# Order of the last stage: a plain tile between two difference jobs, and one quarter's job behind the plain tiles

## The chip, the cores and the metric

The kernel runs on one core of a Trainium2 chip. The metric is the device time of one execution in microseconds; lower is better. The core has TensorE (PE, with its weight loads PEld), VectorE (DVE), ScalarE (ACT), GpSimd (POOL) and SyncE (SP), each with an instruction queue of its own; SyncE issues nearly all DMA transfers.

## The reference

One pre-norm layer for 512 tokens of width 1024, all in float32: a mixing block (attention, pooling and a state-space branch, gated and added to `x`), then a feed-forward block with a short causal convolution, then a last RMSNorm. The change touches only the end:

```python
def conv_ffn(u, w_up, conv_w, conv_b, w_down):
    h = causal_dwconv(u @ w_up, conv_w, conv_b)      # 512 x 5632
    a, v = h[..., :D_FF], h[..., D_FF:]               # D_FF = 2816
    return (jax.nn.silu(a) * v) @ w_down              # 2816 x 1024
...
    x = x + conv_ffn(rmsnorm(x, ln2_g[i]), ...)
return rmsnorm(x, final_g)
```

## The kernel before

**Split products.** Every large product is made in a reduced-precision float format with both operands split in a rounded part and a remainder: `mm3` issues rounded x rounded, rounded x remainder and remainder x rounded weights, in that order (line 234). A weight tile passes through the same steps each time. `fetch` loads it into one of two `raw` buffers (line 183, SyncE). `cast` rounds it in two parts into `wh`, one of three buffers (line 195, ScalarE). `low` subtracts to get the remainder `wl`, one of two buffers (line 215, VectorE); with that `raw` is free again.

**Jobs.** The program is a list of jobs, one for each weight tile, in the order of `program`. Ahead of the body of job n the main loop emits the split of job n+1 (`low`), the rounding of job n+2 (`cast`, with the job's `form` ahead of it, and its two parts emitted in the next calls of `step`) and the load of job n+3 (`fetch`). Each engine runs what it is given in exactly the order in which it is written, so the order of the list sets the order on all queues. `step` also advances the generators in `running`, which emit small pieces of later work.

**The down projection.** The 22 row blocks of `w_down` (128 rows each) are taken in three parts. Two groups of eight blocks are each computed as a 2 x 2 block product with seven products in place of eight, from sums and differences of activation halves and weight quarters (`sevens_down`); the jobs are named `one` to `seven`. The last six blocks are taken plainly (`blocks_of`), once for the left 512 columns (h = 0) and once for the right ones (h = 1): a job with four blocks and one with two, each for four tiles of 128 tokens (tb = 0 to 3). A job of the seven has 2 x 12 matmuls of 512 columns; the plain jobs have 48 and 24.

The second group's jobs `two`, `one`, `five` and `six` stand between and behind the last jobs of the up projection; `seven`, `four` and `three` and the plain jobs make up the last stage, `down`. Jobs `one`, `six`, `seven` and `four` accumulate into the same two banks `X`, one after the other; after each, `plus` (line 1218, VectorE) adds what the banks then hold to a part of the residual `X1[tb, h]`. The difference weights come from `form`, a subtraction by `diff` on VectorE (line 339) ahead of the rounding:

```python
seven = job(q(0, 0), side(3), into(X, "p7", lambda i: [(2 + i, 1)]),
            lambda: diff(seven.raw, W[1], seven.raw))
four = job(q(1, 0), side("A22"), into(X, "p4", lambda i: [(2 + i, 0)]),
           lambda: diff(four.raw, four.raw, W[1]))
```

So `seven` serves the right half's lower quarter (tb 2 and 3, h = 1) and `four` the left half's lower quarter (tb 2 and 3, h = 0). `three` leaves its sums in two further banks, which the right half's plain jobs continue for tb 0 and 1.

**The last norm** needs the sum of squares of both halves of a token tile. `early` emits the left half's part (`norm_early`: squares on ScalarE, line 438; a small row on VectorE, line 461; the product with the norm's weight on GpSimd, line 462) one `step` after the left half of the tile is complete. `norm_late` follows the right half's evacuation (line 1370) tile by tile, and stores the tile (line 1379).

Of the kernel before, what the change touches and what calls it, by code (L numbers as in the profile page):

```python
# [83 lines left out]
def trunk(ctx: ExitStack, tc, out, x, rel_bias, ln1_g, w_in, b_gate, w_a, pool_w, pool_scale, w_b,  # L84
# [26 lines left out]
    def MM(name):  # L111
        return psum.tile([P, S], F32, name=name, tag="mm")

    def SM(name):
        return psum.tile([P, S], F32, name=name, tag="sm")
# [9 lines left out]
    waiting, running = [], []  # L125
# [99 lines left out]
    def wsrc(w, k0, k1, c0, c1):  # L225
        return w[k0 * P:k1 * P, c0:c1].rearrange("(k p) c -> p k c", p=P)
# [111 lines left out]
    def diff(out, a, b):  # L338
        dve.tensor_tensor(out, a, b, OP.subtract)  # L339
        return out  # L340
# [116 lines left out]
    def norm_early(t, g):  # L457

        ss, v0, xg = small("ss", [P, 1]), cpool.tile([P, 1], F32, name=f"v0_{len(V0)}"), T("xg")
        squares(act, t, ss)  # L460
        dve.tensor_scalar(v0, ss, 1.0 / D, EPS, OP.mult, OP.add)
        pool.tensor_tensor(xg, t, g[:, :S], OP.mult)
        V0.append(v0)
        return v0, xg

    def norm_late(t, g, v0, outs, both=False):

        ss, v, sq, r, rt = (small(n, [P, 1]) for n in ("ss", "v", "sq", "r", "rt"))
        squares(act, t, ss)
        xg = T("xg")  # L470
        dve.tensor_tensor(xg, t, g[:, S:], OP.mult)
        dve.scalar_tensor_tensor(v, ss, 1.0 / D, v0, OP.mult, OP.add)
        act.activation(sq, v, AF.Sqrt)
        yield xg
        dve.reciprocal(r, sq)
        dve.scalar_tensor_tensor(rt, r, v, r, OP.mult, OP.mult)
        dve.tensor_scalar(rt, rt, -0.5, 1.5, OP.mult, OP.add)
        if both:
            dve.tensor_tensor(r, r, rt, OP.mult)
            (_, a), (_, b) = outs(xg)  # L480
            dve.tensor_scalar(a, a, r, None, OP.mult)
            act.mul(b, b, r)
            return
        for o, src in outs(xg):
            dve.tensor_scalar(o, src, r, rt, OP.mult, OP.mult)
# [731 lines left out]
    def plus(tb, h, what):  # L1217
        dve.tensor_tensor(X1[tb, h], X1[tb, h], what, OP.add)
# [4 lines left out]
    def second_half(p, tb):  # L1223
        return [t[:, tb * P:(tb + 1) * P] for t in ACTS[2 * p + 1]]

    def sums(j, p, i):
        return [t[:, i * P:(i + 1) * P] for t in FS[j, p]]

    def quarters(g):

        base = g * KG * P
        q = lambda two, h: w_down[base:base + KG * P, h * S:(h + 1) * S].rearrange(
            "(k two p) c -> two p k c", two=2, p=P)[two]
        n2 = KG // 2
        ks = [g * n2 + i for i in range(n2)]

        def product(ps, ws, parts, first, last, again):
            wh, wl = ws
            mm3(ps, lambda k: wh[:, k, :], lambda k: wl[:, k, :], lambda k: parts[k][0],
                lambda k: parts[k][1], range(n2), first, last, flip=True, again=again)  # L1240

        def job(source, side, use, form=None):
            def body(ws):
                for i in range(2):
                    parts = [side(p, i) for p in ks]
                    use(i, lambda ps, first=True, last=True, again=False:
                        product(ps, ws, parts, first, last, again))
                    step()
            j = Job([source] if source is not None else [], n2, S, body)
            j.form = form  # L1250
            if source is None:
                j.load = lambda: None
            return j

        return q, job

    def side(j):
        if j == "A11":
            return first_half
        if j in ("A12", "A22"):  # L1260
            return lambda p, i: second_half(p, i + 2 * (j == "A22"))
        return lambda p, i: sums(j, p, i)

    def into(banks, name, adds, first=False, close=True):
        def use(i, product):
            if first:
                banks[i] = SM(name)
            product(banks[i], first, close, not first)
            for tb, h in adds(i):
                plus(tb, h, banks[i])  # L1270
        return use

    def sevens_down(g, keep=False):

        q, job = quarters(g)
        W, X, Z = [], {}, {}

        def load():
            for h in range(2):
                W.append(ypool.tile([P, 4, S], F32, name="w3", tag="xs"))  # L1280
                sp.dma_start(W[h], q(h, 1))

        two = job(q(1, 0), side("A12"), into(Z, "p2", lambda i: [(i, 0)], True))
        one = job(q(0, 0), side("A11"), into(X, "p1", lambda i: [(i, 0)], True))
        one.then = lambda: diff(W[0], W[0], one.raw)
        five = job(None, side(1), into(Z, "p5", lambda i: [(2 + i, 1)], True), lambda: W[0])
        if keep:
            three = job(q(1, 1), side(4), into(Z, "p3", lambda i: [], close=False))
            six = job(None, side(2), into(X, "p6", lambda i: [(i, 1)]), lambda: diff(W[1], W[1], W[0]))
        else:  # L1290
            three = job(None, side(4), into(Z, "p3", lambda i: [(i, 1)]), lambda: W[1])
            three.then = lambda: diff(W[1], W[1], W[0])
            six = job(None, side(2), into(X, "p6", lambda i: [(i, 1)]), lambda: W[1])
        seven = job(q(0, 0), side(3), into(X, "p7", lambda i: [(2 + i, 1)]),
                    lambda: diff(seven.raw, W[1], seven.raw))
        four = job(q(1, 0), side("A22"), into(X, "p4", lambda i: [(2 + i, 0)]),
                   lambda: diff(four.raw, four.raw, W[1]))
        return load, dict(two=two, one=one, five=five, three=three, six=six, seven=seven, four=four), Z

    def down(rest, opened):  # L1300

        plain = blocks_of(0, {}, (), ())
        yield rest["seven"]
        yield next(plain)
        yield rest["four"]
        yield from plain
        yield rest["three"]
        yield from blocks_of(1, opened, (0, 1), ())

# [53 lines left out]
    def early(tb):  # L1363
        yield
        fin[tb] = norm_early(X1[tb, 0], fin["g"])

    def blocks_of(h, acc, opened, keep):
        def evac(tb, ps):
            t = X1[tb, h]
            dve.tensor_tensor(t, t, ps, OP.add)  # L1370
            if h == 0:
                running.append(early(tb))
                return
            v0, xg0 = fin[tb]
            for _ in norm_late(t, fin["g"], v0, lambda xg1: ((xg1, xg1), (xg0, xg0)),
                               tb == 3):
                xg1 = _
            for i, o in ((1, xg1), (0, xg0)):
                (sp if i or tb < 3 else act).dma_start(out[tb * P:(tb + 1) * P, i * S:(i + 1) * S], o)

        return jobs_b(lambda k0, k1: [wsrc(w_down, KS + k0, KS + k1, h * S, h * S + S)], S,
                      lambda k, tb: ACTS[KS + k][0][:, tb * P:(tb + 1) * P],
                      lambda k, tb: ACTS[KS + k][1][:, tb * P:(tb + 1) * P], KF - KS, evac,
                      mk=(MM, SM)[h], tail=2 if h else 0, acc=acc, opened=opened, keep=keep,
                      again=(0, 1) if h else ())
# [6 lines left out]
    def program():  # L1392
# [34 lines left out]
        for pair in range(2):  # L1427
            for h in range(2):
                yield from wo_jobs(pair, h)
            if pair == 0:  # L1430
                yield Call(ff_cols)
        first, between, _ = sevens_down(0)
        second_, last_, opened = sevens_down(1, keep=True)
        extra = {EARLY + i: between[w] for i, w in enumerate(
            ("two", "one", "five", "three", "six", "seven", "four"))}
# [9 lines left out]
        yield Call(lambda: fin.setdefault("g", grow(final_g)))  # L1445
        yield Call(finish)
        yield from down(last_, opened)

    jobs = list(program())
# [19 lines left out]
    first = [MM("pa") for _ in range(4)]  # L1469
# [57 lines left out]
    banks = [SM("uT") for _ in range(4)]  # L1527
# [137 lines left out]
```

## Time and profile before

| | |
|---|---|
| median of 3 runs | 1039.03 us (1038.7 to 1039.3) |
| profiled execution | 1038.0 us |
| its span | 1036.2 us |
| mean granted TensorE clock | 0.998 |
| TensorE busy | 1024.7 us of the span (99%), 5204 matmuls |
| VectorE, ScalarE, GpSimd busy | 676.2, 473.8, 149.6 us |

The span runs from the first to the last recorded instruction; the execution's own time is 1.8 us longer. All times within the profile are counted from the span's start. Matmuls are pipelined: the next one begins before the last one's recorded end, and a row with "x4" is four in a run. The name after the line is what an instruction writes, and behind the arrow what it reads.

The last stage begins at about 978 us, with job `seven`.

### The profile page before, as it was taken

What the parts mean: (1) busy time and instruction counts of PE and PEld (TensorE: products, weight loads), DVE (VectorE), ACT (ScalarE), POOL (GpSimd) and SP (SyncE); (2) the same over time, 40 slices, a digit from 0 to 9 for tenths busy, and PEclk for the clock granted to TensorE, in tenths of its full rate; (3) what the DMA queues carried; (4) which work ended last, traced back from release to release, by engine and by line L of the source; (5) the groups of instructions that cost most, each with busy time, mean ns of one, the idle gap of its engine ahead of it and who ended that gap; (6) DMA issues with size and microseconds to landing.
All of it is one profiled execution on the core that took longest, in us unless ns stands there. A gap on an engine that the chain in (4) does not pass through costs nothing.

```text
span 1036.2 us, 13090 instructions
## 1 busy us (share of the span) xinstructions
PE 1024.7 (99%) x5204; PEld 859.7 (83%) x5204; DVE 676.2 (65%) x907; ACT 473.8 (46%) x765; POOL 149.6 (14%) x125
## 2 busy tenths in 40 slices
PE   9999999999999999999999999999999999999997
PEld 9898878898888878888888888898888888888785
DVE  6553566684356658766768656766768677666855
ACT  6432544442564364557445324545444443443332
POOL 1770000000000004210152500001111001111110
PEclk9999999999999999999999999999999999999999
DMA  8344312126222344542244525543233224323232
GB/s 280 123 131 134 116 47 75 31 64 200 82 82 82 98 132 115 144 136 69 66 149 153 172 82 204 175 140 114 82 115 122 89 82 163 122 90 114 82 122 82
DMA packets 119069, 120.76 MB, mean 117 GB/s; under 512 B 5316, under 2 KB 101383, under 8 KB 119008
## 3 DMA queue, kind: packets, MB, share of 16 engines
q1 hardware_dynamic: 118415, 119.07, 36.4%
q8 instruction: 41, 0.67, 0.3%
q10 hardware_dynamic: 592, 0.86, 0.2%
q14 instruction: 21, 0.16, 0.1%
HBM read 116.12 MB, written 2.22 MB: 114 GB/s over the span
## 4 chain that ended last, share of the span: by engine, by line
PE 96%; DVE 1%; ACT 1%; DMA 1%; issue 0%; ACTq 0%; DVEq 0%
PE pa L234 35%; PE pu L234 22%; PE pb L234 11%; PE pqk L234 9%; PE p L234 8%; PE pa L1516 2%; PE ps L670 1%; PE pu L1324 1%; PE ppw L234 1%; PE pt L698 1%; PE po L711 1%; PE py L996 1%; DMA xin<-in_x_dram 1%; PE pyo L1003 1%; PE pst L982 0%; PE pxs L950 0%
## 5 line engine op out<-in xcount | busy, mean ns | idle before, releaser
L215 DVE TENSOR_TENSOR wl<-raw,wh 128x2048 fp32r<-128x2048 f32 (+3 forms) x95 | 218.8, 2305 | 50.2 <-ACT wh L195 40.6
L195 ACT CAST wh<-raw 128x1024 fp32r<-128x1024 f32 (+3 forms) x188 | 189.4, 1026 | 68.0 <-DVE raw L339 26.0
L1187 DVE SCALAR_TENSOR_TENSOR hc<-pu,fcol,hc 128x510 f32<-128x510 f32 x88 | 65.8, 747 | 58.9 <-ACT hc L1184 57.3
L234 PE MATMUL pa<-uh,wh 128*128 128x512 f32 x384 | 98.5, 398 | 0.0
L234 PE MATMUL pa<-ul,wh 128*128 128x512 f32 x384 | 94.9, 389 | 0.0
L234 PE MATMUL pa<-uh,wl 128*128 128x512 f32 x384 | 94.9, 389 | 0.0
L234 PEld LDWEIGHTS pa<-ul,wh 128*128 128x128 f32 x384 | 72.1, 188 | 15.2
L234 PEld LDWEIGHTS pa<-uh,wl 128*128 128x128 f32 x384 | 72.1, 188 | 15.0
L234 PE MATMUL pu<-uh,wl 128*128 128x512 f32 (+1 forms) x352 | 83.7, 380 | 0.0
L234 PE MATMUL pu<-uh,wh 128*128 128x512 f32 (+1 forms) x352 | 83.5, 379 | 0.0
L234 PE MATMUL pu<-ul,wh 128*128 128x512 f32 (+1 forms) x352 | 83.5, 379 | 0.0
L234 PEld LDWEIGHTS pa<-uh,wh 128*128 128x128 f32 x384 | 70.3, 188 | 14.7 <-issue 0.7
L234 PEld LDWEIGHTS pu<-uh,wl 128*128 128x128 f32 x352 | 64.1, 188 | 12.8 <-DVE wl L215 0.3
L234 PEld LDWEIGHTS pu<-ul,wh 128*128 128x128 f32 x352 | 64.2, 188 | 12.5
L234 PEld LDWEIGHTS pu<-uh,wh 128*128 128x128 f32 x352 | 64.1, 188 | 12.4
L1192 POOL TENSOR_TENSOR hc<-hc 128x512 f32<-128x512 f32 x22 | 30.5, 1388 | 278.9 <-DVE hc L1187 243.1
L1184 ACT ACTIVATE hc<-pu,fcol,fcol 128x512 f32<-128x512 f32 x40 | 31.2, 780 | 81.3 <-PE pu L234 81.0
L958 POOL TENSOR_TENSOR xd<-xc,dec 128x512 f32<-128x512 f32 x6 | 6.4, 1060 | 334.1 <-DVE xc L952 315.2
L1085 ACT ACTIVATE sg<-pa,col 128x512 f32<-128x512 f32 x24 | 16.5, 688 | 55.3 <-PE pa L234 48.6
L691 ACT ACTIVATE sb<-sb,both 128x128 f32<-128x128 f32 (+1 forms) x72 | 30.1, 419 | 23.5 <-DVE both L688 13.4
L234 PE MATMUL pqk<-uh,wh 128*128 128x512 f32 x144 | 36.9, 394 | 0.0
L234 PE MATMUL pqk<-ul,wh 128*128 128x512 f32 x144 | 36.3, 390 | 0.0
(352 smaller groups left out, 1793.2 us busy)
## 6 DMA issues: line engine op xcount, KB each, us to landing
raw<-in_w_in_dram SPq DMA_DIRECT2D x25, 1024.0 KB
raw<-in_ffn_w_up_dram SPq DMA_DIRECT2D x22, 1024.0 KB
raw<-in_ffn_w_down_dram SPq DMA_DIRECT2D x11, 1024.0 KB
raw<-in_w_in_dram SPq DMA_DIRECT2D x20, 512.0 KB
raw<-in_w_o_dram SPq DMA_DIRECT2D x8, 1024.0 KB
raw<-in_w_b_dram SPq DMA_DIRECT2D x4, 1024.0 KB
al<-ad SPq DMA_DIRECT2D x16, 256.0 KB
w<-in_ffn_w_down_dram SPq DMA_DIRECT2D x4, 1024.0 KB
```

The lines of the kernel that those rows point to most:

```text
L195: act.copy(job.high[:, :, o], job.raw[:, :, o])
L215: (eng or dve).tensor_tensor(l[:, :, o], job.raw[:, :, o], h[:, :, o].bitcast(F32), OP.subtract)
L234: pe.matmul(ps, l, r, start=first and n == 0, stop=last and n == total - 1, skip_group_check=again)
L670: pe.matmul(pss[i][:, o:o + w * P], q[r, n * P:(n + 1) * P], k[r, kb * P:(kb + w) * P], start=True, stop=True)
L691: act.activation(sb[:, off:off + w * P], sb[:, off:off + w * P], AF.Exp, bias=nm[:, n, h:h + 1], accum_out=ls[:, n, h:h + 1])
L698: pe.transpose(pt[:, o:o + P], sb[:, o:o + P], eye)
L711: pe.matmul(po[DH * hh:DH * hh + DH, n * P:(n + 1) * P], V[g, kb + i][:, (2 * cc + hh) * DH:(2 * cc + hh + 1) * DH], probs[2 * cc + hh, mb ...
L1085: act.activation(s, ps, AF.Sigmoid, bias=col[:, o:o + 1])
L1184: act.activation(t, ps, AF.Identity, bias=ff["c1"][:, ff["b"] + m:ff["b"] + m + 1], scale=fw(2, m))
L1187: dve.scalar_tensor_tensor(t[:, sh:], ps[:, :S - sh], fw(k, m), t[:, sh:], OP.mult, OP.add)
L1192: pool.tensor_tensor(a, a, t, OP.mult)
L1516: pe.matmul(first[2 * n + j][:, lo:hi], a[:, k, j * P:(j + 1) * P], b[:, k, lo:hi], start=a is wh and b is uh and k == 0, stop=a is wl and ...
```

## The change

The first plain job of the left half (four blocks, all four token tiles) moves ahead of `seven`, between it and `six`, and `four` moves behind the second plain job. The order of the last stage becomes

| | |
|---|---|
| before | (six) seven, plain 4, four, plain 2, three, right half |
| after | (six) plain 4, seven, plain 2, four, three, right half |

Loads, casts, differences and splits move with their jobs. Since the left halves of tiles 2 and 3 are now completed by `four`, its `plus` and no longer the plain evacuation hands those two tiles to `early`.

```diff
-    def into(banks, name, adds, first=False, close=True):
+    def into(banks, name, adds, first=False, close=True, final=False):
...
             for tb, h in adds(i):
                 plus(tb, h, banks[i])
+            if final:
+                running.append(early(2 + i))
...
-        four = job(q(1, 0), side("A22"), into(X, "p4", lambda i: [(2 + i, 0)]),
+        four = job(q(1, 0), side("A22"), into(X, "p4", lambda i: [(2 + i, 0)], final=keep),
                    lambda: diff(four.raw, four.raw, W[1]))
...
         plain = blocks_of(0, {}, (), ())
+        yield next(plain)
         yield rest["seven"]
-        yield next(plain)
+        yield from plain
         yield rest["four"]
-        yield from plain
         yield rest["three"]
         yield from blocks_of(1, opened, (0, 1), ())
...
             if h == 0:
-                running.append(early(tb))
+                if tb < 2:
+                    running.append(early(tb))
                 return
```

## The prediction

> **What bounds the kernel now.** I read the page first, then TensorE's waits, then a table of stretches of the last stage, then its timeline engine by engine, because the page only says that TensorE is the bound and not where it loses time.
>
> ```profile
> span 1036.2 us, 13090 instructions
> PE 1024.7 (99%) x5204; PEld 859.7 (83%) x5204; DVE 676.2 (65%) x907; ACT 473.8 (46%) x765; POOL 149.6 (14%) x125
> ```
>
> TensorE is busy for 99% of the span, so a change of order can only win back its few gaps. TensorE's waits from 840 to 1030 us are a single row (time, count, longest), and the stretches cut at the job borders (length, then busy us and instructions of PE, PEld, DVE, ACT, POOL; granted clock; DMA share; GB/s) show the same gap:
>
> ```profile
> PE p L234 <- DVE x L1218: 1.7, 1, 1.7
> ...
> 978.16:980.04 1.88, 0.16 (x2) 0.03 (x1) 1.88 (x3) 0.59 (x1) 0.00 (x0) 1.00 0.00 0
> 980.04:985.60 5.56, 5.56 (x25) 4.58 (x25) 4.36 (x4) 0.00 (x0) 0.00 (x0) 1.00 0.72 236
> 985.60:996.48 10.88, 10.88 (x50) 9.01 (x48) 4.67 (x4) 3.11 (x5) 0.00 (x0) 1.00 0.35 122
> 996.48:1012.58 16.10, 16.10 (x73) 13.33 (x72) 10.88 (x13) 7.64 (x14) 6.89 (x4) 1.00 0.30 98
> 1012.58:1029.30 16.72, 16.70 (x74) 13.51 (x72) 10.37 (x25) 4.07 (x10) 0.20 (x1) 1.00 0.17 65
> 1029.30:1036.20 6.90, 0.00 (x0) 0.00 (x0) 2.72 (x8) 1.65 (x4) 0.00 (x0) 0.72 0.39 150
> ```
>
> Between 978.16 and 980.04 TensorE does nothing but drain; from 980.04 to 1029.30 it has no gap at all, and the clock is 1.00 on both sides. What remains after 1029.30 is the last tile's norm and its store. The timeline at the gap says who is late (start, length, engine, line, operation, count, and in brackets the idle time before):
>
> ```profile
> 972.72 1.07 PE L234 MATMUL p<-wh,sah 128*128 128x512 f32 x4
> ...
> 977.25 1.07 PE L234 MATMUL p<-wl,sah 128*128 128x512 f32 x4
> 980.04 1.17 PE L234 MATMUL p<-wh,sbh 128*128 128x512 f32 x4 [1.72 <-DVE x L1218]
> ...
> 985.60 1.07 PE L234 MATMUL pb<-wh,fh 128*128 128x512 f32 x4
> ...
> 969.41 2.29 DVE L339 TENSOR_TENSOR raw<-w,raw 128x2048 f32<-128x2048 f32 x1
> 971.61 1.53 DVE L1187 SCALAR_TENSOR_TENSOR hc<-pu,fcol,hc 128x510 f32<-128x510 f32 x2
> ...
> 975.30 0.69 DVE L1200 TENSOR_TENSOR fl<-hc,fh 128x512 fp32r<-128x512 f32 x1
> 975.91 3.38 DVE L215 TENSOR_TENSOR wl<-raw,wh 128x2048 fp32r<-128x2048 f32 x1
> ...
> 979.22 0.67 DVE L1218 TENSOR_TENSOR x<-x,p 128x512 f32<-128x512 f32 x1
> ...
> 973.60 1.04 ACT L195 CAST wh<-raw 128x1024 fp32r<-128x1024 f32 x1
> 974.65 0.62 ACT L1199 CAST fh<-hc 128x512 fp32r<-128x512 f32 x1
> ```
>
> Job "six" (sah) runs from 972.72. Job "seven" (sbh) accumulates into the same two banks (`X`), so its first matmul must wait until `plus` (L1218) has read six's first bank. The bank is complete at about 975.5, when three of six's six groups are done, but in VectorE's queue `plus` stands behind the split of seven's weights (L215, 975.91 to 979.29) and ends only at 979.89.
>
> **The change, part by part.** *The gap.* A job of 24 matmuls takes 5.44 us where nothing disturbs it, one of 48 takes 10.88; the chain of waits (start, length, what) has both:
>
> ```profile
> 956.56 5.44 PE p L234 x24
> ...
> 985.76 10.88 PE pb L234 x48
> 996.64 5.44 PE p L234 x24
> 1002.08 5.44 PE pb L234 x24
> ```
>
> Six could hand over at 972.72 + 5.44 = 978.16. Seven starts at 980.04, which is 1.88 us late, and itself takes 985.60 - 980.04 = 5.56, that is 0.12 more than 5.44, since the pipe has to fill again. So the gap costs 2.00 us. After the change the first plain job follows six. It writes four banks of its own (`pb`), does not need `X`, and its inputs, activations 16 to 19, were split long before. What it needs is its weights. Its rounded half is cast where seven's was (second part at 973.60), and its remainder is now the subtraction at VectorE's same place: behind the row at 975.30, ready at 979.29. The first remainder matmul is the ninth, after 8 x 5.44/24 = 1.81 us, at 979.97. That leaves 0.68 us of slack, so no wait: minus 2.00 us. The work itself, 24 + 48 + 24 + 24 matmuls, is unchanged.
>
> *Seven, one job later.* Its difference (L339, 2.29) leaves the place at 969.41 and stands behind the plain job's subtraction, 979.29 to 981.6; the `hc` row at 971.61 comes some 2 us earlier, which nobody waits for. Then come seven's first cast on ScalarE (1.04, to 982.6) with the last activation's cast queued behind it, six's two `plus` (to 984.5), the second cast (984.2), and seven's subtraction to about 986.9. Seven now starts at 978.16 + 10.88 = 989.04 and needs the remainder at 990.85: 4 us of slack. The plain job covers all of this; without such cover it would cost 986.9 - 979.97 = 7 us.
>
> *The loads.* Two raw buffers alternate, so each load starts when a subtraction frees its buffer. The issues on SyncE and what landed:
>
> ```profile
> 979.37 0.37 SPq L183 DMA_DIRECT2D raw<-in_ffn_w_down_dram  x1
> 983.32 0.37 SPq L183 DMA_DIRECT2D raw<-in_ffn_w_down_dram  x1
> ...
> 984.49 2.29 DVE L339 TENSOR_TENSOR raw<-raw,w 128x2048 f32<-128x2048 f32 x1 [1.20 <-DMA raw<-in_ffn_w_down_dram]
> 991.25 0.37 SPq L183 DMA_DIRECT2D raw<-in_ffn_w_down_dram  x1
> 996.41 2.00 ACT L195 CAST wh<-raw 128x1024 fp32r<-128x1024 f32 x2 [6.47 <-DMA raw<-in_ffn_w_down_dram]
> 1005.04 0.37 SPq L183 DMA_DIRECT2D raw<-in_ffn_w_down_dram  x1
> 1008.76 0.62 ACT L195 CAST wh<-raw 128x512 fp32r<-128x512 f32 x1 [1.78 <-DMA raw<-in_ffn_w_down_dram]
> ```
>
> So 1 MB is usable 5.12 to 5.16 us after its issue, half of that after 3.72. SyncE's queue keeps its length; only who takes which buffer changes. After the change the second plain job's load (0.5 MB) goes at 979.3 and lands at 983.0. Job four's load goes at 986.9, behind seven's subtraction, and lands at 992.1, when VectorE has nothing else urgent: its difference ends at 994.4, its two casts (2.00) at 996.4, its subtraction at 998.8. Four starts at 989.04 + 5.44 + 5.44 = 999.92 and needs the remainder at 1001.73: slack 2.9. Queued behind four's difference on VectorE are seven's two `plus`, and behind its subtraction the four evacuations of the plain jobs; their readers come later than 1001.7. The second plain job's own remainder waits only for a buffer that the first plain job frees at 989.0, and is needed at 994.48 + 0.9.
>
> *The norm's first half.* Tiles 2 and 3 now finish with four's `plus` instead of the plain evacuation, so their squares move behind four, while tiles 0 and 1 stay where they were. The rows that price this:
>
> ```profile
> 1005.64 0.63 ACT L438 ACTIVATE junk<-x 128x512 f32<-128x512 f32 x1 [0.59 <-DVE x L1370]
> 1005.69 7.10 POOL L462 TENSOR_TENSOR xg<-x,grow 128x512 f32<-128x512 f32 x4 [28.54 <-DVE x L1370]
> ...
> 1007.56 0.69 DVE L1370 TENSOR_TENSOR x<-x,pb 128x512 f32<-128x512 f32 x1 [0.67 <-PE pb L234]
> ...
> 1008.29 3.34 DVE L215 TENSOR_TENSOR wl<-raw,wh 128x2048 fp32r<-128x2048 f32 x1
> ```
>
> Four ends at 1005.36 and three at 1010.80, 2.00 us earlier than before. Job three's load goes at 990.4, lands by 997 and is split from 1001.9, behind four's split and the plain evacuations (four at 0.69, the last at 1001.6), to 1005.3, taking 3.34 if GpSimd's products lie beside it; needed at 1007.2. The right half's first load goes at 998.8 and lands at 1004.0; its casts end at 1006.0; tile 2's square (0.63) is queued behind them on ScalarE, tile 2's small `v0` row waits for it on VectorE, and behind that stands the right half's subtraction: from 1007.1, by 1010.5 at 3.34. It is needed at 1010.80 + 1.81 = 1012.6. The last half-load goes at 1005.3, lands at 1009.0, is cast around tile 3's square by 1011 and split by 1012.4; needed at 1010.80 + 2.72 + 0.9 = 1014.4. The thinnest slack is 2.0 us. I take nothing for all this; the bounds are nothing below, since unbroken matmuls can't be done earlier, and the second rival's price above.
>
> *A rule that speaks against it.* GpSimd's two products at the gap lie beside VectorE's work:
>
> ```profile
> 973.31 1.30 POOL L1192 TENSOR_TENSOR hc<-hc 128x512 f32<-128x512 f32 x1 [28.92 <-DVE hc L1187]
> 975.44 1.71 POOL L1192 TENSOR_TENSOR hc<-hc 128x512 f32<-128x512 f32 x1 [0.82 <-ACT fh L1199]
> ```
>
> The subtraction took 3.38 beside the second product, against 2.29 for the like-sized row at 969.41. The Trainium skill, page "SBUF — State Buffer", section "Who interferes with whom", says that a VectorE instruction with two SBUF inputs and a GpSimd instruction that reads SBUF exclude each other for a whole instruction. By that rule a further product beginning ahead of the subtraction's turn would hold it up once more; the first rival has that time, from rows. The row's extra 1.09 fits one such block, and no run shows two.
>
> *Sum.* -2.00 on TensorE, nothing elsewhere, the same tail: span 1036.2 - 2.0 = 1034.2, the profiled execution 1038.0 - 2.0 = 1036.0. The three timed runs have a median of 1039.03 (1038.7 to 1039.3), 1.0 above the profiled one; from it 1037.03. I predict 1037.0.
>
> **Rivals.** *A new wait takes part of the gain.* If both products fall on the plain job's subtraction, it ends some 1.3 later, at 980.6, and TensorE waits 0.6 plus a refill of 0.12: gain 1.3, time 1037.7. Against: the first product is freed by the `hc` row that now comes earlier, at about 971, away from it.
>
> *Loads too slow, the time ends above.* After the change the loads of four and three are issued 3.5 us apart, and each later one hangs on the split before it. If a load needed L instead of 5.2 us, four's split would end at 998.8 + (L - 5.2), the right half's load would start there and take L, and its casts (2.00) and its split (2.29) would follow; that split is needed at 1012.6. It costs from 2L = 14.7, at some 7.4 us a load, and every further 1 us of L costs 2. The gain is gone at 8.4. With two loads sharing the DMA engines and each taking 10.4, it loses 6.1 and wins 2.0: 1043.1. Against: the load of 979.37 had another one issued 4 us behind it and still landed in 5.12, and the DMA share in these stretches is 0.30 to 0.35.
>
> *The gap only moves.* If six's banks are not what the first matmul waits for, but something common to any next job, as the remainder's subtraction, the plain job would stall as well: 1039.0. Against: the row names L1218, and the subtraction ends before its ninth matmul.
>
> **How the numbers follow.** The forecast has 0.82, the first rival 0.07, slow loads 0.07, the moved gap 0.04. A measurement of this kernel tells about 0.2% from no change, 2.08 us here, so the line lies at 1036.95, and the forecast of 2.00 stands almost on it; the timed runs spread by 0.3 to each side, and the profiled one lies lower than all three. I split the forecast's 0.82 into 0.44 beyond the line and 0.38 within. Within go also the first and third rivals: 0.49. Slower is 0.07. The range runs from the sum on the profiled execution, 1036.0, less 0.2, to the first rival with the runs' spread, 1038.1; it leaves out slow loads, the moved gap and some scatter.
>
> **What would show it.** Right: no wait of TensorE between six and the first plain job, the plain job's first matmul at about 978.2, seven's at 989.0, four's at 999.9, three's at 1005.4, the last matmul some 2.0 earlier, near 1027.3, and the same 6.9 us after it. Wrong: a TensorE wait before four or the right half put down to a cast or a load (slow loads), one inside the first plain job put down to L215 (first rival), or a tail longer than 6.9 because the norms of tiles 2 and 3 came late.

## The result and the profile after

| | before | after |
|---|---|---|
| median of 17 runs each | 1038.70 us (1038.12 to 1041.57) | 1036.44 us (1035.82 to 1038.72) |
| ratio | | 0.9979, 95% interval 0.9972 to 0.9986 |
| span of the profiled execution | 1036.2 us | 1034.5 us |
| from six's first matmul to the end of the last one | 56.57 us | 54.57 us |

The change makes the kernel faster by 0.21%. The last row is the cleanest reading: 1029.29 - 972.72 before, 1027.58 - 973.01 after. The ends come from the last TensorE rows of the two chains of waits (start, length, what; before, then after):

```profile
1021.12 8.17 PE pb L234 x36
...
1019.41 8.17 PE pb L234 x36
```

The stage is shorter by exactly the 2.00 us of the gap. The span fell by 1.7 only because six began 0.29 us later in this execution, which goes back to the first microseconds and not to the change. TensorE's waits over the whole span after have a third row of 0.7 where before it was 0.3, and no row of the last stage at all:

```profile
PE pa L1476 <- DVE relb L523: 1.1, 1, 1.1
PE pcb L927 <- ACT xcv L1015: 1.0, 1, 1.0
PE uT L1536 <- DVE diag L1548: 0.7, 1, 0.7
PE po L711 <- ACT sb L699: 0.2, 1, 0.2
PE pxs L950 <- DVE o L716: 0.2, 1, 0.2
```

The page's head, and the stretches of the last stage after (length, then busy us and instructions of PE, PEld, DVE, ACT, POOL; clock; DMA share; GB/s):

```profile
span 1034.5 us, 13089 instructions
PE 1024.3 (99%) x5204; PEld 859.9 (83%) x5204; DVE 676.0 (65%) x907; ACT 473.8 (46%) x765; POOL 149.2 (14%) x125
...
978.16:989.04 10.88, 10.88 (x49) 9.01 (x49) 7.60 (x6) 3.57 (x5) 0.00 (x0) 1.00 0.23 69
989.04:994.48 5.44, 5.44 (x25) 4.51 (x25) 3.73 (x3) 0.11 (x1) 0.00 (x0) 1.00 0.86 298
994.48:1000.00 5.52, 5.52 (x26) 4.55 (x26) 4.66 (x6) 4.46 (x7) 0.63 (x1) 1.00 0.26 58
1000.00:1005.40 5.40, 5.40 (x25) 4.49 (x24) 4.67 (x6) 2.21 (x5) 2.51 (x3) 1.00 0.52 189
1005.40:1010.80 5.40, 5.40 (x25) 4.48 (x24) 3.17 (x4) 2.83 (x7) 3.77 (x2) 1.00 0.25 94
```

TensorE's busy time equals the length in every stretch, where before 1.72 of 1.88 us were empty. The timeline after, at the old gap and at the splits on which the forecast's slacks rest (a selection of rows, so some between them are left out):

```profile
973.01 1.07 PE L234 MATMUL p<-wh,sah 128*128 128x512 f32 x4
...
976.09 3.38 DVE L215 TENSOR_TENSOR wl<-raw,wh 128x2048 fp32r<-128x2048 f32 x1
...
978.45 1.07 PE L234 MATMUL pb<-wh,fh 128*128 128x512 f32 x4
979.39 2.28 DVE L339 TENSOR_TENSOR raw<-w,raw 128x2048 f32<-128x2048 f32 x1
980.26 1.07 PE L234 MATMUL pb<-wl,fh 128*128 128x512 f32 x4
981.59 0.67 DVE L1218 TENSOR_TENSOR x<-x,p 128x512 f32<-128x512 f32 x1
984.57 2.29 DVE L215 TENSOR_TENSOR wl<-raw,wh 128x2048 fp32r<-128x2048 f32 x1
989.33 1.07 PE L234 MATMUL p<-wh,sbh 128*128 128x512 f32 x4
991.97 2.29 DVE L339 TENSOR_TENSOR raw<-raw,w 128x2048 f32<-128x2048 f32 x1 [1.16 <-DMA raw<-in_ffn_w_down_dram]
996.40 2.29 DVE L215 TENSOR_TENSOR wl<-raw,wh 128x2048 fp32r<-128x2048 f32 x1 [0.75 <-ACT wh L195]
1000.21 1.07 PE L234 MATMUL p<-wh,fh 128*128 128x512 f32 x4
...
1002.02 1.07 PE L234 MATMUL p<-wl,fh 128*128 128x512 f32 x4
1005.65 1.07 PE L234 MATMUL p<-wh,sbh 128*128 128x512 f32 x4
1006.58 2.28 DVE L215 TENSOR_TENSOR wl<-raw,wh 128x2048 fp32r<-128x2048 f32 x1
...
1012.90 1.07 PE L234 MATMUL p<-wl,fh 128*128 128x512 f32 x4
```

The plain job follows six at 978.45 without a wait, and six's first addition, now at 981.59, has nobody waiting for it until seven at 989.33. The plain job's split (976.09) is as long as seven's was and ends at 979.47, 0.79 us ahead of the matmul at 980.26.

### The profile page after: what moved, and what is told of

Read it like the earlier page. It is cut to its first block, busy times and chain, and to the rows that moved or that the text cites. A ratio compares the mean times of both kernels' runs of the same rounds, so it can differ in the third digit from the quotient of the medians.

```text
span 1034.5 us, 13089 instructions
## 1 busy us (share of the span) xinstructions
PE 1024.3 (99%) x5204; PEld 859.9 (83%) x5204; DVE 676.0 (65%) x907; ACT 473.8 (46%) x765; POOL 149.2 (14%) x125
## 4 chain that ended last, share of the span: by engine, by line
PE 97%; DVE 1%; ACT 1%; DMA 1%; issue 0%; ACTq 0%; DVEq 0%
PE pa L234 35%; PE pu L234 22%; PE pb L234 11%; PE pqk L234 9%; PE p L234 8%; PE pa L1519 2%; PE ps L670 1%; PE pu L1326 1%; PE ppw L234 1%; PE pt L698 1%; PE po L711 1%; PE py L996 1%; DMA xin<-in_x_dram 1%; PE pyo L1003 1%; PE pst L982 0%; PE pxs L950 0%
```

## Experiments

The theory: seven waited for a bank that VectorE had not read yet, because that read was queued behind a split; whatever gets the read out of the way, or stands between six and seven for long enough, wins the same 2.0 us, and the place of four is free. The rivals: four's place and the norm's later start matter; or the split itself was what seven waited for. All ratios are to the kernel before on the same chip; the intervals are some 0.0009 to each side, so sub-microsecond verdicts rest on the traces.

**The changed kernel again.**

> The changed kernel again, beside the others of this group. Theory: 2.0 us below the kernel before (ratio 0.9981), no wait of TensorE from 840 us to the last matmul. Rival (part of the gain of the first runs was scatter): 1 us or less.

Measured 0.9980 (0.9971 to 0.9989): 1036.13 against 1038.09, no TensorE wait from 840 us to the last matmul, and 54.57 us from six to the last matmul.

**The plain job first, four left in place.**

```diff
+        yield next(plain)
         yield rest["seven"]
-        yield next(plain)
         yield rest["four"]
         yield from plain
```

> The first part alone: the four-block plain job moves between six and seven, job four stays ahead of the second plain job, so four follows seven directly, and the norm of tiles 2 and 3 starts where it did. Theory (the gap is the bank that seven shares with six, and any job that covers VectorE's backlog wins it): the whole 2.0 us, ratio 0.9981, no TensorE wait between six and the end. Four uses the same banks as seven, but its split is queued ahead of seven's first addition only until about 991.6 and its load lands at 984.5, so four starts without a wait. Rival (the place of four matters too, by its load or by the norm's first half): a gap of 0.5 to 1.9 us opens between seven and four, or the time falls by less than 1 us.

Measured 0.9982 (0.9974 to 0.9991), 1036.34 us. The chain of waits of this kernel (start, length, what) runs on without a break, seven and four as one piece of 48, and it is 54.57 us from six to the last matmul:

```profile
973.75 5.44 PE p L234 x24
979.19 10.88 PE pb L234 x48
990.07 10.88 PE p L234 x48
1000.95 5.44 PE pb L234 x24
```

The whole gain is there, so four's move has no part in it.

**Four behind the plain tiles, seven left in place.**

```diff
         yield rest["seven"]
-        yield next(plain)
-        yield rest["four"]
         yield from plain
+        yield rest["four"]
```

As in the whole change, four then hands tiles 2 and 3 to `early`.

> The second part alone: seven stays right behind six, and four moves behind the second plain job, with the norm of tiles 2 and 3 started from it. Theory: the gap of 1.9 us between six and seven stays, so no change (ratio 1.000, within 0.4 us). Rival (the later place of four gives part of the gain): 0.5 to 1 us faster; or (the later norm costs) slower by up to 1 us.

Measured 1.0002 (0.9993 to 1.0011), 1038.23 us, and TensorE's only wait in the stage is the old one:

```profile
PE p L234 <- DVE x L1218: 1.7, 1, 1.7
```

The first two runs split the change: its first half is worth all of it, its second nothing.

**The order of before, the bank read ahead of the split.**

```diff
                     use(i, lambda ps, first=True, last=True, again=False:
                         product(ps, ws, parts, first, last, again))
+                    if i == 0 and j.late:
+                        j.prepare()
                     step()
...
+        six.late = keep
```

While six runs, `prepare` emits the split of the next job's weights, those of seven.

> The order of before; only the place of one split on VectorE changes: while six runs, its first addition is queued ahead of the split of seven's weights instead of behind it. Theory (the wait is the queue order on VectorE): the addition ends at about 976.7, seven's split at about 979.5 to 980.0, seven's first matmul follows six without a gap or with one of up to 0.3 us, and the time falls by 1.7 to 2.0 us (ratio 0.998). Rival (seven's weights are as late as the bank, so the split is the real bound): the split now ends later by the addition's 0.7 us, TensorE waits for it instead, and less than 1 us is won.

Measured 0.9984 (0.9976 to 0.9993), 1036.40 us. Its timeline:

```profile
976.30 0.68 DVE L1218 TENSOR_TENSOR x<-x,p 128x512 f32<-128x512 f32 x1
976.90 2.79 DVE L215 TENSOR_TENSOR wl<-raw,wh 128x2048 fp32r<-128x2048 f32 x1
...
978.54 1.07 PE L234 MATMUL p<-wh,sbh 128*128 128x512 f32 x4
979.44 1.07 PE L234 MATMUL p<-wh,sbl 128*128 128x512 f32 x4
```

No job has moved, and the gap is gone all the same: 54.57 us from six to the last matmul. The split ends later than in the kernel before counted from six's start (6.59 against 6.57 us) and TensorE does not mind, so the split was never the bound. The queue order on VectorE was.

**The last product off GpSimd.**

```diff
-        pool.tensor_tensor(a, a, t, OP.mult)
+        if m < 2 * KF - 1:
+            pool.tensor_tensor(a, a, t, OP.mult)
 
-        def later():
+        def later(v=t):
             yield
             k = m - KF
+            if k == KF - 1:
+                dve.tensor_tensor(a, a, v, OP.mult)
```

> The order of before; the very last product of the up projection, which GpSimd makes beside the split of seven's weights, is made by VectorE instead, right behind six's first addition. Theory (the gap is the split's length plus the addition, and GpSimd's product stretches the split): the split takes 2.3 instead of 3.38 us, the gap shrinks from 1.88 to 0.8 us, the time falls by 1.0 (ratio 0.999). Rival (the split's length is not what seven waits for): the gap stays at 1.9 us and the time does not move.

Measured 0.9991 (0.9982 to 1.0000), 1037.07 us against 1038.18. The timeline at the gap:

```profile
975.90 2.29 DVE L215 TENSOR_TENSOR wl<-raw,wh 128x2048 fp32r<-128x2048 f32 x1
978.10 0.68 DVE L1221 TENSOR_TENSOR x<-x,p 128x512 f32<-128x512 f32 x1
...
978.93 1.16 PE L234 MATMUL p<-wh,sbh 128*128 128x512 f32 x4 [0.63 <-DVE x L1221]
```

The wait is 0.63 instead of 1.72: 1.09 us, the amount by which the split shrank. So more than half of the gap, 1.09 of 2.00 us, was GpSimd's product, felt by TensorE through a split that it was not waiting for.

**Three as the cover.**

```diff
+        yield rest["three"]
         yield rest["seven"]
...
         yield from plain
-        yield rest["three"]
```

> The order of before with job three, which uses other banks, moved between six and seven: a cover of 24 matmuls (5.44 us) instead of 48 (10.88 us). Theory (the cover must outlast seven's backlog: its split ends at about 986.9, and with this cover seven starts at 983.6 and needs it at 985.4): no wait behind six, but one of 1.0 to 1.6 us in front of or inside seven, put down to the cast or the split of its weights; the time falls by 0.5 to 1.0 us. Rival (any job that does not use the two banks is enough): the whole 2.0 us.

Measured 0.9992 (0.9984 to 1.0001), 1037.40 us. TensorE now waits twice at seven (timeline):

```profile
984.16 1.21 PE L234 MATMUL p<-wh,sbh 128*128 128x512 f32 x4 [0.28 <-ACT wh L195]
985.21 1.09 PE L234 MATMUL p<-wh,sbl 128*128 128x512 f32 x4
986.73 1.19 PE L234 MATMUL p<-wl,sbh 128*128 128x512 f32 x4 [0.44 <-DVE wl L215]
```

With 24 matmuls as cover seven's cast and then its split come late. The two waits add up to 0.72 us, less than the 1.0 to 1.6 expected, but the rows behind them are longer too (1.21 and 1.19 us where 1.07 is usual), and seven is done 1.33 us late: 55.90 us from six to the end, so 0.67 of the 2.00 is left. Thus 24 matmuls are too few here, and the plain job's 48 are enough; nothing between was tried.

**Four's split made longer.** The subtraction of four's remainder is made twice with the same values, and in other runs three times (`four.times = 3`):

```diff
-            (eng or dve).tensor_tensor(l[:, :, o], job.raw[:, :, o], h[:, :, o].bitcast(F32),
-                                       OP.subtract)
+            for _ in range(getattr(job, "times", 1)):
+                (eng or dve).tensor_tensor(l[:, :, o], job.raw[:, :, o], h[:, :, o].bitcast(F32),
+                                           OP.subtract)
...
+            four.times = 2
```

> The same subtraction made twice: 2.3 us more on VectorE. Theory: inside the slack of 3.3 us, no TensorE wait from six to the last matmul, and the span from six's first matmul to the last one is that of the changed kernel (54.6 us). Rival (no slack): a wait of about 2 us before or inside four.

Measured: 1036.00 us in a single execution, no TensorE wait from 840 us on, 54.71 us from six to the last matmul. The slack was used up here: the second subtraction ended at 1001.51 and its reader began at 1001.59. Timed afterwards:

> The changed kernel with four's subtraction made twice, now timed. Theory (slack of 3.3 us, and the long executions belong to the TensorE wait that the third subtraction brings): all executions within 1035.6 to 1036.9, ratio 0.998, none at a mean clock of 0.997. Rival (the extra work of VectorE alone brings the long executions): some of them near 1038.5, 2 to 3 us above the rest, at a lower mean clock.

Measured 0.9986 (0.9977 to 0.9995), 1036.55 us (1036.07 to 1038.05). No execution at a mean clock below 0.998 and no wait in its trace, but four of the eleven lay between 1037.48 and 1038.05, above the range that I gave. So the theory's range was missed, and the rival's lower clock did not show either. In the trace the doubled subtraction runs from 996.42 to 1001.04, and its reader comes at 1001.94: 2.3 us of VectorE work cost nothing there.

> The changed kernel with the subtraction of four's split made three times over (the same values each time), which puts 4.6 us more on VectorE ahead of four. Theory (that split has a slack of about 3.3 us: it ended at 998.7 and its ninth matmul came at 1002.0): TensorE waits some 1.3 us inside four, nothing later, and 0.5 to 0.8 us of the gain is left. Rival (no slack: VectorE's backlog goes straight into the time): 2.6 us slower than the kernel before.

Measured 1.0009 (1.0000 to 1.0018): a median of 1039.13, from 1037.43 to 1040.91. That is 0.95 us above the kernel before, where a gain of 0.5 to 0.8 us was expected. The trace alone is as expected:

```profile
996.21 6.94 DVE L216 TENSOR_TENSOR wl<-raw,wh 128x2048 fp32r<-128x2048 f32 x3 [0.95 <-ACT wh L195]
...
1003.21 1.21 PE L235 MATMUL p<-wl,fh 128*128 128x512 f32 x4 [1.44 <-DVE wl L216]
```

The profiled execution took 1037.66 us, with one wait of 1.44 and none after it. Five of the eleven executions took 1040.2 to 1040.9, however, all with a mean granted clock of 0.997 where the others have 0.998 or 0.999. One more kernel was made for that, and the kernel with three subtractions was run again:

```diff
+            for _ in range(getattr(job, "more", 0)):
+                (eng or dve).tensor_tensor(l[:, :, o], l[:, :, o].bitcast(F32),
+                                           l[:, :, o].bitcast(F32), OP.max)
...
+            four.more = 2
```

> The changed kernel with the same 4.6 us of extra work on VectorE in front of four's remainder being ready, but behind the subtraction that frees the load buffer: the subtraction is made once, and two instructions of its size then rewrite the remainder with its own values. TensorE waits inside four as with the subtraction made three times (about 1.4 us), but the right half's first load goes out 4.6 us earlier. In that run the profile had 0.5 us of the gain left, while 8 of 11 timed executions took 0.8 to 3.3 us more, five of them 2.5 to 3.3 us more at a lower mean clock. Theory A (the right half's split, with 0.3 us of slack left there, is late in those executions because its load or its casts are): with the earlier load all executions lie within 1037.3 to 1038.3. Theory B (the wait inside four itself brings the clock down in some executions): the same mixture, about half of the executions near 1040.

Measured 1.0006 (0.9997 to 1.0015), 1037.34 to 1040.42. The load was freed after a single subtraction and TensorE waited 1.38 us inside four:

```profile
996.39 2.29 DVE L215 TENSOR_TENSOR wl<-raw,wh 128x2048 fp32r<-128x2048 f32 x1 [0.91 <-ACT wh L195]
998.71 4.62 DVE L218 TENSOR_TENSOR wl<-wl 128x2048 fp32r<-128x2048 f32 x2
...
1003.38 0.97 PE L237 MATMUL p<-wl,fh 128*128 128x512 f32 x3 [1.38 <-DVE wl L218]
```

Three of eleven executions were at 0.997 and took 1039.9 to 1040.4. The right half's first load went out at 998.71 instead of 1003.23, so theory A falls as it was put. The last half-load, however, went out no earlier (1008.77 against 1008.60), and its split had 0.8 us to spare; that this load is late in the long executions is not excluded.

> The kernel with the subtraction made three times again, on the same chip as the one before. Theory A and B alike: the mixture of 1037.4 to 1040.9 comes back. If the profiled execution is a long one, theory A expects a TensorE wait in front of or inside the right half's first job put down to a load, a cast or a split; theory B expects no further wait but a stretch after 1003 us with a granted clock below 1.

> One more profile of the same kernel, for the chance of a long execution; expectations as for the run before it.

Measured 1.0016 (1.0007 to 1.0026), 1040.06 us; five of nine executions at 0.996 or 0.997, the longest 1043.09. The two profiled executions were short ones (1038.58 and 1038.33 us), with one wait of 1.8 and 1.7 us inside four and a clock of 1.00 in every stretch after it. So no long execution was seen from within: that the wait inside four lowers the clock in part of the executions is in line with the counts (13 of 31 with that wait, none of the eleven with two subtractions and no wait). Where the clock falls, and that the wait causes it, was not shown, and this stays open.

## Why the prediction was right

**The gap.** The step that carried the forecast, 1.88 us late plus 0.12 of refill, measured 2.00: 56.57 - 54.57. The plain job needed nothing that was late; its split's slack was 0.79 where 0.68 was forecast. The listed signs came too, each some 0.3 later because six began 0.29 later: the plain job at 978.45, seven at 989.33, four at 1000.21, three at 1005.65, the end of the last matmul at 1027.58, and 6.9 us behind it as before. Two runs separate the cause from its rivals: with only the bank's read moved up the gap went as well, and with a shorter split it shrank by as much as the split.

**The number.** 1037.0 was built on the median of three runs, 1039.03. With seventeen the kernel before stands at 1038.70, so a third of a microsecond of the 0.6 between forecast and result came from that base; the rest, 2.26 between the medians where the trace has 2.00, is within the runs' scatter (1.96 in the second group). The result lies on the line of 0.2%, as the forecast said: 0.21% in the first group, 0.20% in the second. On which side of the line it fell was luck, and the chances left it open (0.44 beyond, 0.49 within).

**Seven, one job later.** Its split was forecast to end at 986.9 and ended at 986.86; seven's remainder matmul followed at 991.14, a slack of 4.3 where 4 was forecast. "Without such cover it would cost 7 us" was not tried; half the cover cost 1.33 (2.00 - 0.67).

**The loads.** Four's load was forecast to land at 992.1 and its split to end at 998.8; they came at 991.97 and 998.69. The slack in front of four, forecast 2.9, was 3.3 (998.69 to 1002.02). The longer splits bear that out roughly: 2.3 us more fitted, and 4.65 us more made the remainder's matmul 1.5 to 2.0 us late, which leaves 2.7 to 3.1; the execution with only 0.08 us left behind the doubled subtraction had 2.4. The slow-load rival had nothing to work on: four's load, issued at 986.88, came in 5.1 us after its buffer was free. Three's, issued at 990.84, hardly shared the DMA engines with it, since the rate fell from 401 to 102 GB/s between the two, at about 992, and rose to 403 again; together they make the DMA share of 0.86 in 989 to 994 us.

**The norm's first half.** These terms were mis-sized, on the safe side. By the forecast's own figures the thinnest slack was job three's, 1007.2 - 1005.3 = 1.9, and not the 2.0 that it states, which is the last half-load's (1014.4 - 1012.4). The timeline after has three's split, the last half-load's, and the matmul that needs each:

```profile
1001.14 2.94 DVE L215 TENSOR_TENSOR wl<-raw,wh 128x2048 fp32r<-128x2048 f32 x1
...
1007.46 1.07 PE L234 MATMUL p<-wl,sbh 128*128 128x512 f32 x4
...
1011.34 1.23 DVE L215 TENSOR_TENSOR wl<-raw,wh 128x1024 fp32r<-128x1024 f32 x1 [2.17 <-PE p L234]
...
1014.72 0.61 PE L234 MATMUL p<-wl,fh 128*128 128x512 f32 x2
```

Three's split had 3.4 us. The right half's first split, forecast at 3.34 beside GpSimd, took 2.28 (row 1006.58) and ended 4.0 us ahead of the matmul at 1012.90. The last half-load's split had 2.15, close to the 2.0 of the forecast but for another reason: it waited 2.17 us for TensorE, as three's last remainder matmuls (1010.18 + 1.07) then free a `wl` buffer, a wait that the forecast does not have. After the change GpSimd's product was the one held up (3.06, below).

**The first rival** (two products on one split) did not come about: the first product ran at 971.39, when VectorE's `hc` row had moved up as forecast, and the split met one product as before (GpSimd's timeline after):

```profile
971.39 1.29 POOL L1192 TENSOR_TENSOR hc<-hc 128x512 f32<-128x512 f32 x1 [26.71 <-DVE hc L1187]
975.73 1.59 POOL L1192 TENSOR_TENSOR hc<-hc 128x512 f32<-128x512 f32 x1 [3.05 <-DVE hc L1187]
```

The run without GpSimd's last product gives the price of one: 1.09 us. **The moved gap** is refuted by the timeline and by the run with only the queue order changed. **What the prediction did not see** is that the second half of the change is worth nothing by itself (1.0002): it moved along without cost, which is what "I take nothing" said, but no step of the forecast asked whether it was needed. The runs showed a smaller cure besides: the read moved up in VectorE's queue won the same 2.00 us.

## What to carry to other kernels

When a matmul waits for a bank, look at what stands ahead of the bank's reader in that reader's queue: the reader's data may have been there for microseconds (here 3.7, from 975.5 to 979.2). Then the cheapest cure is to move the read up in its queue, which won as much here as reordering whole jobs. A job used as cover must outlast the backlog behind it, so compare its length with the end of the late job's last preparation, and test each half of a change alone, since one half may do nothing.

## What the runs showed of the hardware

A VectorE subtraction of two 128x2048 operands takes 2.29 us alone. Beginning while GpSimd's product ran, it took 3.38 (before and after the change), 2.79 when it began 0.6 us later into the same product (with the bank read ahead of it), and 2.29 with the product taken away. The extra 1.09 and 0.50 us are a little less than what was left of the product when the subtraction began, 1.24 and 0.64 by GpSimd's rough ends (977.15 and 977.54). In the kernel after, a product that began behind a subtraction (1006.58) was the one to wait, 3.06 us where an undisturbed one takes 1.30 (GpSimd's timeline):

```profile
1004.81 1.30 POOL L462 TENSOR_TENSOR xg<-x,grow 128x512 f32<-128x512 f32 x1 [2.89 <-DVE x L1218]
1006.96 3.06 POOL L462 TENSOR_TENSOR xg<-x,grow 128x512 f32<-128x512 f32 x1 [0.84 <-POOL xg L462]
```

The Trainium skill, page "SBUF — State Buffer", section "Who interferes with whom", states that a VectorE instruction with two SBUF inputs contends with a GpSimd instruction that reads SBUF, that their shared port pair is an exclusive lock, and that the order of issue decides who blocks; the rows of both orders agree with it, as far as GpSimd's rough ends allow.

The kernels with a TensorE wait of 1.4 to 1.8 us in the middle of job four had a lower mean clock (0.996 or 0.997) in 13 of 31 executions; these took 1039.9 to 1043.1 us, the others 1037.3 to 1039.4. In the 94 executions of the kernel before that ran beside the experiments, with a wait of 1.7 us between two jobs, no mean clock was below 0.998 and the longest took 1039.57. But among the first seventeen of that kernel two took 1040.95 and 1041.57, with no clock on record, and the kernel after, with no such wait, had one execution in seventeen at 0.997, its longest (1038.72). So the wait goes with the long executions more often, and is not shown to cause them. I had expected a wait of this length to cost its length and the refill, and did not find out why more came of it.
